# One modulation group on TensorE and early loads for another, in the lead-in of a two-layer hybrid decoder trunk

## The chip, the cores and the metric

The kernel runs on one core of a Trainium2 chip. The core has engines that run side by side, each with its own instruction stream: PE (TensorE, matrix products; the trace lists its weight loads apart, as PEld), DVE (VectorE), ACT (ScalarE), POOL (GpSimd), and SP, which here only issues transfers (DMA). The metric is the device time of one execution in microseconds (us), less is better. Three executions of the kernel before took 2290.22 to 2292.53 us, with a median of 2290.46.

## The reference

Two layers over x of 1024 tokens by 1024 channels, then a final RMSNorm. What matters for the change is the head of a layer:

```python
c_act = jax.nn.silu(c)                       # one conditioning vector of 1024
mod = c_act @ w_ada + b_ada                  # 3072 numbers for each layer
shift, scale, gate = jnp.split(mod[:, None, :], 3, axis=-1)
h = rms_norm(x, norm_g) * (1.0 + scale) + shift
proj = h @ w_in                              # all inputs of the three mixers
...                                          # pooling, retention, RWKV-7, merge
return x + gate * (merged @ w_out)
```

So no product of the first layer can start before the shift and scale of at least some channels are there, and `w_ada`, a matrix of 1024 by 3072, has to be multiplied by a single vector for them.

## The kernel before

x lies transposed: eight tiles of 128 channels (kt = 0 to 7), in two halves of 512 tokens each (h = 0, 1). A product of float32 accuracy is made from three fast ones: both operands are split into a high and a low part (hhi, hlo for the normalised x; two parts of a weight tile), and high by high, low by high and high by low are added up in PSUM.

The lead-in (`lead_in`, lines 1809 to 1895) brings the first layer to the point where its first three items, the columns called lora, k and r of head 0, are projected. `mms(h, kt)` makes the nine products of one x tile with those three items; 16 such calls, 144 products, are the lead-in's work on PE. They add up in six PSUM accumulators: three of the pool `acc` for h = 0, and `ch` and the two banks of `two` for h = 1. Before `mms(h, kt)` can run, `normed(h, kt)` (DVE) multiplies the x tile by the token's inverse root mean square, `affine(h, kt)` (ACT, two instructions) applies scale and shift for hhi and for x itself, and `low` (POOL) makes hlo. The sums over squares that the root mean square needs are `sq(h)`: ACT squares, DVE adds, PE sums over partitions by products with a column of ones. `rstd` and `rstd_bc` make the inverse root and spread it over a PSUM bank, from which `normed` reads. `one(h, kt)` is all of it for one tile.

Shift and scale come from six modulation groups. Groups 0 to 3 hold the shift and scale of x tiles 0, 1, 2 and 3, with four weight tiles of 128 x 512 each; groups 4 and 5 those of tiles 4, 5 and 6, 7, with eight weight tiles each. A group is computed by `ada` (line 695): eight steps on DVE, one for each 128 rows of `w_ada`, each of which multiplies a weight tile by a number per partition and adds it to a running sum in PSUM (`ada_ps`, the last step writes `ada_acc`). Then PE sums over the partitions with one-column products into `sums`, a PSUM bank shared by all these little sums (`small`, line 688), and `ada_end` makes `mod` and `acoef` on DVE. `coef(g)` runs a whole group. There is a second way, `ada_columns` (line 722), which the kernel before defines and, with `COLUMNS = ()`, doesn't use: PE multiplies each 128 x 128 block of the weights by a column of c, adds over the eight blocks in PSUM, and DVE has only `ada_end` to do.

The weight tiles of the groups live in borrowed buffers. Groups 0 and 1 fill the eight slots of a ring in tile G (`wada_slot`, the names `ringG`). Groups 2 and 3 use the `wh` and `wl` buffers, three of each, so that the last two of their eight tiles wait until group 2 has read its first two (`wada`). Group 4 takes the ring again as groups 0 and 1 free it (`aload(4, 8)`), and group 5 takes each ring slot as group 4 frees it: `astep(4, 5)` issues one step of group 4 and then one load for group 5. Other buffers of the lead-in: `ri` has 14 tiles, seven of which hold x of the second half; `r8` has four tiles of 128 x 2048, three of which hold the split weights of the first three items (`wbig`). The fourth `r8` tile is taken at the lead-in's end by `wprep(True)`, for the split weights of the next item. Raw weights arrive in three `wr` buffers.

The order of the work is not that of the code. Every call is recorded as an `Op` in `Log`, with its dependencies; a PSUM tensor counts by whole banks (`pieces`, line 157). `Log.plan` (line 333) then plays the whole program with assumed durations, transfers included, and picks at each point, for each engine, the ready operation with the lowest key, which is its place in the code plus a bias for its kind. Operations of the lead-in and of the RWKV chain count as urgent; a pending urgent one can hold back a longer one that isn't. A buffer is given in the order in which the code asks for it, once its earlier user is done. Some subtractions may be given to DVE or POOL, whichever is free by the plan. `emit` writes the instructions in the order of planned start times, each engine's and SP's queue included, and since `emit` issues them all, nearly every instruction has line 539 in the profile; the tile names tell them apart. The rope tables (`ang`, `nrot`, `over`), a job of DVE for the retention mixer, are not urgent and are slipped in where DVE is free by the plan.

Of the kernel before, what the change touches and what calls it, by code (L numbers as in the profile page):

```python
# [9 lines left out]
F32 = mybir.dt.float32  # L10
# [7 lines left out]
P = 128  # L18
# [4 lines left out]
HF = 512  # L23
# [67 lines left out]
    ADA.append((_c, [_c + _i for _i in range(4)], _n))  # L91
    _n += 8
FIRST = [("lora",), ("k", 0), ("r", 0)]
COLUMNS = ()
TWICE = (1, 2)
EARLY = (0, 0, 0, 2, 4)


# [454 lines left out]
def trunk_kernel(ctx, tc, xT, cvec, pos, vecs, consts, w_ada, w_all, pool_w, lora_w, out):  # L553
    nc = Log(tc.nc, tc)

    def pool(name, bufs, **kw):
        return PoolProxy(nc, ctx.enter_context(tc.tile_pool(name=name, bufs=bufs, **kw)), bufs, "")
# [3 lines left out]
    wp = pool("wp", 2)  # L561
# [18 lines left out]
    def nm(s):  # L580
        uid[0] += 1
        return f"{s}_{uid[0]}"

    def slot(tag, n, w=HF):
        def f(s, dt=F32):
            return (tp if w == HF else mp).tile([P, w], dt, tag=tag, name=nm(s), bufs=n)

        return f
# [3 lines left out]
    t_ri = slot("ri", 14)  # L592
# [24 lines left out]
    def r8(s):  # L617
        return rp.tile([P, 2048], F32, tag="r8", name=nm(s))
# [53 lines left out]
    def cond_act():  # L672
        cth = sp.tile([P, 8], F32, tag="mn", name=nm("cth"))
        nc.scalar.activation(cth, cact, AF.Tanh, scale=0.5)
        nc.vector.tensor_scalar(cth, cth, 0.5, 0.5, op0=ALU.mult, op1=ALU.add)
        nc.vector.tensor_tensor(cact, cact, cth, op=ALU.mult)
        nc.scalar.activation(fixed[:, 3:4], ones, AF.Sqrt)

    def ada_load(l, g, slot_, ws, n):
        for _ in range(n):  # L680
            w = slot_("wada")
            nc.sync.dma_start(out=w, in_=w_ada[l, ADA[g][2] + len(ws)])
            ws.append(w)

    sums_ps = []
    aw = [[] for _ in range(6)]

    def small(n):
        if not sums_ps:
            sums_ps.append([mx("sums"), 0])  # L690
        t, o = sums_ps[0]
        sums_ps[0][1] = o + n
        return t[:, o : o + n]

    def ada(l, g, slot_, gap=2200, acc_=t_lt, ws=None):
        n = len(ADA[g][1])
        W_ = n * P
        acc = acc_("ada_acc")[:, 0:W_]
        late = ws is None
        ws = [] if late else ws  # L700
        part = acc if late else mx("ada_ps")[:, 0:W_]
        for kt in range(NKT):
            i, o = divmod(kt * W_, HF)
            if late and o == 0:
                ada_load(l, g, slot_, ws, min(i + 2, 2 * n) - len(ws))
            w = ws[i][:, o : o + W_]
            if kt == 0:
                nc.vector.tensor_scalar_mul(part, w, cact[:, 0:1])
            else:
                nc.vector.scalar_tensor_tensor(  # L710
                    part if kt < NKT - 1 else acc, w, cact[:, kt : kt + 1], part, op0=ALU.mult, op1=ALU.add
                )
            yield gap
        if late:
            yield wait(acc)
        ps = mx("adaps") if late else small(n)
        for m in range(n):
            mmul(ps[:, m : m + 1], acc[:, m * P : (m + 1) * P], ones)
        ada_end(l, g, ps)
        yield  # L720

    def ada_columns(g):
        c, cols, _ = ADA[g]
        n = len(cols)
        ps = small(n)
        for m in range(n):
            for kt in range(NKT):
                i, o = divmod(kt * n * P, HF)
                mmul(
                    ps[:, m : m + 1], aw[g][i][:, o + m * P : o + m * P + P], cact[:, kt : kt + 1],  # L730
                    start=kt == 0, stop=kt == NKT - 1,
                )
        ada_end(0, g, ps)
# [233 lines left out]
    def plan_layer(l):  # L967
# [4 lines left out]
        while done < 4 or prog.get((l, 3), 0) < 10 or pools:  # L972
# [7 lines left out]
            elif pools and 4 - len(pools) <= done and len(lanes["mix"]) < 2:  # L980
                yield from pools.popleft()
            elif 24 - len(gates) < EARLY[done]:
                yield gates.popleft()
# [68 lines left out]
    def acc_ps():  # L1052
        return ps_a.tile([P, HF], F32, tag="acc", name=nm("acc"))
# [655 lines left out]
    def xdma(h, *kts):  # L1709
        for kt in kts:  # L1710
            xt = (mi if h == 0 else t_ri if kt < 7 else t_rk)("x")
            nc.sync.dma_start(out=xt, in_=xT[kt, h])
            xin[h].append(xt)
# [3 lines left out]
    def sq(h, *kts):  # L1717
        for kt in kts:
            t = mo("sq")
            nc.scalar.square(t, xin[h][kt])  # L1720
            if kt == 0:
                ssp[h] = small(4)
            if kt == 0 and TWICE[h] or kt % 2 == 0 and TWICE[h] == 1:
                prev = t
                continue
            if TWICE[h]:
                nc.vector.tensor_tensor(t, t, prev, op=ALU.add)
                prev = t
            if TWICE[h] == 2 and kt < 7:
                continue  # L1730
            for m in range(4):
                mmul(
                    ssp[h][:, m : m + 1], t[:, m * P : (m + 1) * P], ones,
                    start=kt == (1, 7)[TWICE[h] - 1] and m == 0, stop=kt == 7 and m == 3,
                )
# [22 lines left out]
    def normed(h, *kts, eng=None):  # L1758
        for kt in kts:
            if (h, kt) in isnorm:  # L1760
                continue
            isnorm.add((h, kt))
            x = xin[h][kt]
            if eng is None:
                nc.vector.tensor_tensor(x, x, rbc[h], op=ALU.mult)
            else:
                eng.tensor_tensor(x, x, rbs[h], op=ALU.mult)

    def affine(h, kt):
        x = xin[h][kt]  # L1770
        b, a = mod[0][:, SHIFT[kt] : SHIFT[kt] + 1], acoef[0][:, kt : kt + 1]
        hi, lo = hb("hhi"), hb("hlo")
        nc.scalar.activation(hi, x, AF.Identity, bias=b, scale=a)
        nc.scalar.activation(x, x, AF.Identity, bias=b, scale=a)
        h_cur[h].append((hi, lo))

    def low(eng, h, kt):
        hi, lo = h_cur[h][kt]
        eng.tensor_tensor(lo, xin[h][kt], hi.bitcast(F32), op=ALU.subtract)
# [3 lines left out]
    def wdma(j, *tiles):  # L1783
        for i in tiles:
            if j == 0:
                wbig.append(r8("wbig"))
            wraw[j, i] = wp.tile([P, HF], F32, tag="wr", name=nm("wr"), bufs=3)
            nc.sync.dma_start(out=wraw[j, i], in_=w_all[0, i, j])
# [16 lines left out]
    def steps(g, n):  # L1805
        for _ in range(n):
            next(g)

    def lead_in():
        V, G_ = nc.vector, nc.gpsimd  # L1810
        gs = [ada(0, g, None, ws=aw[g]) for g in range(6)]

        def aload(g, n):
            ada_load(0, g, wada_slot, aw[g], n)

        def both(kt, eng=None):
            for h in range(2):
                affine(h, kt)
                low(eng or G_, h, kt)

        def astep(g, nxt=None):
            for _ in range(8):
                steps(gs[g], 1)
                if nxt is not None:
                    aload(nxt, 1)

        cond_act()
        xdma(0, *range(8))
        nc.sync.dma_start(out=vec[0][:, 0:NVEC], in_=vecs[0])
        aload(0, 4)  # L1830
        nc.sync.dma_start(out=cst, in_=consts[:, 0 : CST["bone"]])
        wdma(0, 0)
        xdma(1, 0, 1, 2, 3)
        wdma(0, 1, 2)
        aload(1, 4)
        xdma(1, 4, 5, 6, 7)
        for g, n in ((2, 4), (3, 4)):
            for _ in range(n):
                w = wp.tile([P, HF], F32, tag=("wh", "wl")[_ % 2], name=nm("wada"), bufs=3)
                ada_load(0, g, lambda _: w, aw[g], 1)  # L1840
        def coef(g):
            if g in COLUMNS:
                ada_columns(g)
            else:
                steps(gs[g], 9)

        def one(h, kt):
            normed(h, kt)
            affine(h, kt)
            low(G_, h, kt)  # L1850
            mms(h, kt)

        acc6[0] = [acc_ps() for _ in range(3)]
        derive(0)
        sq(0, *range(8))
        rstd(0)
        rstd_bc(0)
        coef(0)
        wsp(0, 0, 1, 2)
        one(0, 0)  # L1860
        coef(1)
        one(0, 1)
        sq(1, *range(8))
        rstd(1)
        rstd_bc(1)
        coef(2)
        acc6[1] = [ps_c.tile([P, HF], F32, tag="ch", name=nm("acc")), cyt(), cyt()]
        normed(0, *range(3, 8))
        one(0, 2)
        wdma(1, 0, 1, 2)  # L1870
        aload(4, 8)
        normed(1, *range(8))
        one(1, 0)
        one(1, 1)
        coef(3)
        one(0, 3)
        one(1, 2)
        wsp(1, 0, 1, 2)
        astep(4, 5)
        steps(gs[4], 1)  # L1880
        one(0, 4)
        one(1, 3)
        one(0, 5)
        coef(5)
        one(1, 4)
        one(0, 6)
        one(1, 5)
        one(0, 7)
        one(1, 6)
        one(1, 7)  # L1890
        wprep(True)
        wprep()
# [486 lines left out]
```

## Time and profile before

| | |
|---|---|
| median of three executions | 2290.46 us |
| profiled execution | 2293.27 us |
| its span, first to last instruction | 2291.2 us |
| PE, PEld busy | 2249.2 us (98%), 1865.2 us (81%) |
| DVE, ACT, POOL busy | 1633.0 us (71%), 910.5 us (40%), 624.3 us (27%) |
| mean granted clock of TensorE | 0.993 |
| moved by DMA | 248.84 MB, 109 GB/s over the span |

All numbers below this table come from one profiled execution, on its own clock that starts with the span. The profile gives busy times for stretches of the span, lists instructions in order of time with the idle time ahead of each and what ended it, and groups instructions by the names of their output and inputs: `acc<-hhi,wbig` is a product of hhi with a weight tile of wbig into an accumulator. `x8` means eight records in a row. A product of plain float32 operands stands as two records. A busy PE isn't PE at its peak, since products overlap; the ends are modelled, and starts are the better measure of their rate. The granted clock is a share of TensorE's full rate.

### The profile page before, as it was taken

Reading aid. Unit: us, or ns where it says so; the run is one execution under the profiler, and the core shown is the slowest. Engines: PE = TensorE matmul, PEld = TensorE weight load, DVE = VectorE, ACT = ScalarE, POOL = GpSimd, SP = SyncE. Lnnn points to the kernel's source line nnn. Section 1 sums busy time; section 2 is a strip of 40 time slices with the busy share of each in tenths; the row PEclk is TensorE's granted clock in tenths of the full one; section 3 lists DMA queues with packets and bytes.
Section 4 is the critical chain, followed back from the end, with each engine's and each line's share of the span. In section 5 each row is a group of like instructions: output and inputs, shape, how many; then the busy total and the mean of one; then the engine's idle time right before and its main releaser. Section 6 shows DMA issues by size and latency. Waiting matters only on the chain.

```text
span 2291.2 us, 35095 instructions
## 1 busy us (share of the span) xinstructions
PE 2249.2 (98%) x13048; PEld 1865.2 (81%) x13048; DVE 1633.0 (71%) x2911; ACT 910.5 (40%) x1673; POOL 624.3 (27%) x549
## 2 busy tenths in 40 slices
PE   6999999999999999999999999999999999999998
PEld 5788888888888888888888888887888888888888
DVE  7996886878888754668667778688785844465854
ACT  5743433434234344323454344243432444442243
POOL 4132323323325210322122232332432500041311
PEclk8999999999999999999999999999999999999999
DMA  8221111112356642755540111111122533257442
GB/s 303 94 56 55 33 47 33 53 47 75 120 160 196 220 138 88 234 180 167 166 147 28 47 33 39 56 39 47 47 68 82 188 119 112 88 163 231 132 132 83
DMA packets 138042, 248.84 MB, mean 109 GB/s; under 512 B 15632, under 2 KB 18960, under 8 KB 137872
## 3 DMA queue, kind: packets, MB, share of 16 engines
q1 hardware_dynamic: 137872, 246.61, 33.3%
q8 instruction: 102, 1.67, 0.3%
q14 instruction: 68, 0.56, 0.1%
HBM read 187.04 MB, written 59.51 MB: 108 GB/s over the span
## 4 chain that ended last, share of the span: by engine, by line
PE 89%; DVE 5%; issue 1%; ACT 1%; POOL 0%; DVEq 0%; POOLq 0%
PE acc L539 74%; PE two L539 3%; PE ch L539 3%; PE av L539 1%; PE g L539 1%; PE ro L539 1%; PE bt L539 1%; PE rkv L539 1%; PE m L539 1%; DVE G L539 1%; PE lw L539 1%; PE rs L539 0%; PE pps L539 0%; DVE two L539 0%; DVE tm L539 0%
## 5 line engine op out<-in xcount | busy, mean ns | idle before, releaser
L539 PE MATMUL acc<-hhi,wh 128*128 128x512 f32 x1488 | 599.1, 403 | 0.0
L539 PE MATMUL acc<-hlo,wh 128*128 128x512 f32 x1488 | 598.5, 402 | 0.0
L539 PE MATMUL acc<-hhi,wl 128*128 128x512 f32 x1488 | 596.1, 401 | 0.0
L539 POOL TENSOR_TENSOR wl<-wr,wh 128x512 fp32r<-128x512 f32 x175 | 237.1, 1356 | 568.1 <-ACT wh L539 469.8
L539 PEld LDWEIGHTS acc<-hhi,wl 128*128 128x128 f32 x1488 | 280.9, 189 | 50.0 <-issue 1.1
L539 PEld LDWEIGHTS acc<-hhi,wh 128*128 128x128 f32 x1488 | 280.5, 189 | 50.4 <-issue 1.5
L539 PEld LDWEIGHTS acc<-hlo,wh 128*128 128x128 f32 x1488 | 280.8, 189 | 48.8 <-issue 0.7
L539 ACT CAST wh<-wr 128x512 fp32r<-128x512 f32 x242 | 149.2, 617 | 292.2 <-PE acc L539 234.7
L539 PE MATMUL acc<-T,wh 128*128 128x512 f32 x576 | 177.3, 389 | 0.0
L539 PEld LDWEIGHTS acc<-T,wh 128*128 128x128 f32 x576 | 108.1, 188 | 22.4
L539 DVE TENSOR_TENSOR wl<-wsum,wh 128x512 fp32r<-128x512 f32 x75 | 54.0, 720 | 93.3 <-ACT wh L539 92.9
L539 ACT COPY y<-two 64x128 f32<-64x128 f32 x128 | 32.9, 257 | 214.5 <-PE two L539 211.1
L539 PE MATMUL acc<-T,wl 128*128 128x512 f32 x288 | 112.1, 389 | 0.0
L539 DVE SCALAR_TENSOR_TENSOR S<-ch,pc,SP 64x64 f32<-64x64 f32 x256 | 72.0, 281 | 55.3 <-PE ch L539 49.1
L539 POOL TENSOR_TENSOR oz<-ol,oz 128x512 fp32r<-128x512 f32 x10 | 14.0, 1397 | 327.6 <-DVE wl L539 258.9
L539 ACT CAST wh<-wsum 128x512 fp32r<-128x512 f32 x96 | 59.6, 620 | 96.5 <-PE acc L539 93.5
L539 DVE TENSOR_TENSOR xst<-two,MT 64x128 f32<-64x128 f32 x128 | 37.5, 293 | 69.9 <-PE two L539 47.1
L539 DVE TENSOR_TENSOR two<-two,tm 64x30 f32<-64x30 f32 (+14 forms) x240 | 78.9, 329 | 7.0
L539 DVE TENSOR_TENSOR tm<-MT,two 64x30 f32<-64x30 f32 (+14 forms) x240 | 76.4, 318 | 8.5 <-ACT two L539 1.6
L539 DVE TENSOR_TENSOR wl<-wraw,wh 128x512 fp32r<-128x512 f32 x53 | 36.6, 690 | 62.4 <-ACT wh L539 62.4
L539 PE MATMUL acc<-oy,wh 128*128 128x512 f32 x256 | 79.7, 392 | 0.0
L539 PE MATMUL acc<-oG,wh 128*128 128x512 f32 x256 | 79.0, 390 | 0.0
(326 smaller groups left out, 4907.2 us busy)
## 6 DMA issues: line engine op xcount, KB each, us to landing
wr<-in_w_all SPq DMA_DIRECT2D x268, 256.0 KB, 2.7
wraw<-in_w_all SPq DMA_DIRECT2D x96, 256.0 KB, 2.7
gd<-gsg SPq DMA_DIRECT2D x96, 256.0 KB, 2.0
gs<-gd SPq DMA_DIRECT2D x96, 256.0 KB, 4.0
wada<-in_w_ada SPq DMA_DIRECT2D x72, 256.0 KB, 3.0
ol<-od SPq DMA_DIRECT2D x48, 256.0 KB, 3.5
traw<-hd SPq DMA_DIRECT2D x32, 256.0 KB, 3.0
ringG<-in_w_ada SPq DMA_DIRECT2D x24, 256.0 KB, 5.2
```

Of the source, the lines that this page charges most:

```text
L539: o.inst = f(*a, **k)
```

## The change

Three things change, all in the lead-in of the first layer. Group 1 is computed by `ada_columns` on PE instead of by eight steps on DVE. The last two weight tiles of group 3 get `ri` tiles in place of `wh` and `wl` ones. And the eight weight tiles of group 5 get buffers of their own, the fourth `r8` tile cut in four and four more `ri` tiles, with their loads issued right behind those of group 4; group 4's steps then run without loads between them. The ring in G serves groups 0, 1 and 4 only.

```diff
-COLUMNS = ()
+COLUMNS = (1,)
 TWICE = (1, 2)
+SPARE = ((3, 2), (3, 3))
...
         for g, n in ((2, 4), (3, 4)):
             for _ in range(n):
-                w = wp.tile([P, HF], F32, tag=("wh", "wl")[_ % 2], name=nm("wada"), bufs=3)
+                w = t_ri("wada") if (g, _) in SPARE else wp.tile([P, HF], F32, tag=("wh", "wl")[_ % 2], name=nm("wada"), bufs=3)
                 ada_load(0, g, lambda _: w, aw[g], 1)
...
         one(0, 2)
         wdma(1, 0, 1, 2)
         aload(4, 8)
+        more = r8("wada")
+        more = [more[:, i * HF : (i + 1) * HF] for i in range(4)] + [t_ri("wada") for _ in range(4)]
+        for w in more:
+            ada_load(0, 5, lambda _: w, aw[5], 1)
         normed(1, *range(8))
         one(1, 0)
         one(1, 1)
...
         one(1, 2)
         wsp(1, 0, 1, 2)
-        astep(4, 5)
-        steps(gs[4], 1)
+        steps(gs[4], 9)
         one(0, 4)
```

What group 1 now runs, unchanged from the kernel before:

```python
def ada_columns(g):
    c, cols, _ = ADA[g]
    n = len(cols)
    ps = small(n)
    for m in range(n):
        for kt in range(NKT):
            i, o = divmod(kt * n * P, HF)
            mmul(
                ps[:, m : m + 1], aw[g][i][:, o + m * P : o + m * P + P], cact[:, kt : kt + 1],
                start=kt == 0, stop=kt == NKT - 1,
            )
    ada_end(0, g, ps)
```

## The prediction

> **What bounds the kernel now.** I read the page first, then busy time by stretches, because the change touches only the first 80 us.
>
> ```profile
> span 2291.2 us, 35095 instructions
> 20.00:62.00 42.00, 30.93 (x109) 23.94 (x110) 37.45 (x75) 21.59 (x33) 21.71 (x19) 0.79 0.86 302
> 62.00:80.00 18.00, 18.00 (x78) 14.73 (x77) 17.03 (x30) 14.48 (x24) 3.09 (x8) 0.92 0.42 147
> 80.00:140.00 60.00, 57.85 (x353) 46.10 (x352) 56.65 (x85) 37.47 (x58) 14.38 (x14) 1.00 0.10 29
> 140.00:2291.20 2151.20, 2132.34 (x12468) 1770.85 (x12466) 1511.76 (x2697) 824.43 (x1540) 581.06 (x499) 1.00 0.33 105
> 28.00:44.00 16.00, 13.80 (x40) 10.81 (x41) 12.37 (x30) 9.57 (x16) 9.44 (x9) 0.50 0.93 337
> 90.00:120.00 30.00, 29.16 (x157) 22.97 (x156) 29.76 (x42) 19.29 (x29) 7.42 (x7) 1.00 0.11 31
> ```
>
> The columns are the stretch, its length, the busy time of PE, PEld, DVE, ACT and POOL, the granted clock, the DMA share and GB/s. From 62 us to the end PE is busy almost throughout: it idles 2.15 us in 80 to 140 and 2151.20 - 2132.34 = 18.86 us in all the rest. Between 20 and 62 it idles 11.07 us. So what comes off the end of the lead-in should come off the total, unless later work hands it back. The place for it is the stretch 20 to 62, where DVE is busy 37.45 of 42 us. The instructions there, in order of time, tell why PE waits:
>
> ```profile
> 20.69 2.92 PE L539 MATMUL acc<-hhi,wbig 128*128 128x512 f32 x6 [1.63 <-ACT hhi L539]
> 25.30 0.61 PE L539 MATMUL sums<-fixed,ada_acc 128*128 128x1 f32 x4 [0.82 <-DVE ada_acc L539]
> 28.29 0.59 PE L539 MATMUL sums<-fixed,sq 128*128 128x1 f32 x2 [2.39 <-DVE sq L539]
> 52.43 2.06 PE L539 MATMUL acc<-hhi,wbig 128*128 128x512 f32 x7 [2.03 <-ACT hhi L539]
> 61.47 2.93 PE L539 MATMUL acc<-hhi,wbig 128*128 128x512 f32 x6 [3.00 <-ACT hhi L539]
> 64.19 1.15 PE L539 MATMUL acc<-hlo,wbig 128*128 128x512 f32 x3
> 65.18 1.30 PE L539 MATMUL acc<-hhi,wbig 128*128 128x512 f32 x5
> 70.65 1.83 PE L539 MATMUL acc<-hhi,wbig 128*128 128x512 f32 x7
> 72.32 0.39 PE L539 MATMUL two<-hhi,wbig 128*128 128x512 f32 x1
> ...
> 80.02 0.62 PE L539 MATMUL two<-hlo,wbig 128*128 128x512 f32 x2
> ...
> 19.70 0.48 DVE L539 TENSOR_SCALAR ada_ps<-ringG,fixed 128x256 f32<-128x256 f32 x1
> ...
> 27.36 0.15 DVE L539 SCALAR_TENSOR_TENSOR acoef<-mod,vec 128x1 f32<-128x1 f32 x1
> ...
> 34.33 0.18 DVE L539 RECIPROCAL rn<-rn 128x4 f32<-128x4 f32 x1 [1.15 <-ACT rn L539]
> 36.68 1.28 DVE L539 TENSOR_TENSOR x<-x,two 128x512 f32<-128x512 f32 x2 [0.75 <-PE two L539]
> 39.74 0.69 DVE L539 TENSOR_TENSOR x<-x,two 128x512 f32<-128x512 f32 x1 [0.81 <-PE two L539]
> 41.31 2.48 DVE L539 TENSOR_TENSOR x<-x,two 128x512 f32<-128x512 f32 x4 [0.89 <-DMA hd<-x]
> 43.71 0.48 DVE L539 TENSOR_SCALAR ada_ps<-wada,fixed 128x256 f32<-128x256 f32 x1
> 45.16 3.10 DVE L539 SCALAR_TENSOR_TENSOR ada_ps<-wada,fixed,ada_ps 128x256 f32<-128x256 f32 x6
> 57.16 0.75 DVE L539 TENSOR_SCALAR ada_ps<-ringG,fixed 128x512 f32<-128x512 f32 x1
> 60.40 0.16 DVE L539 SCALAR_TENSOR_TENSOR acoef<-mod,vec 128x2 f32<-128x2 f32 x1
> 60.48 2.33 DVE L539 SCALAR_TENSOR_TENSOR ada_ps<-ringG,fixed,ada_ps 128x512 f32<-128x512 f32 x3
> 64.60 0.75 DVE L539 SCALAR_TENSOR_TENSOR ada_acc<-ringG,fixed,ada_ps 128x512 f32<-128x512 f32 x1
> ```
>
> The number in brackets is idle time ahead of the instruction and what ended it. DVE runs the modulation groups one after another: group 3 from 43.71, group 4 behind it, group 5 from 57.16 to 64.60 + 0.75 = 65.35. Group 4's coefficients stand at 60.56, ACT makes the first operand from them, and PE, which had waited 3.00 us, starts at 61.47 on the 36 products of x tiles 4 and 5, then runs without a gap through the 36 of tiles 6 and 7, of which the last lie at 80.02. So the DVE chain up to group 4 sets the end of the lead-in; group 5 is just in time behind it (its steps begin with no wait at 57.16).
>
> **Group 1 to PE.** On DVE eight steps of 128x256 go. Six such steps took 3.10 us (45.16), 0.517 each: 8 x 0.517 = 4.1 us off the chain ahead of coef(4). They lay between 19.70 and the sums at 25.30; the chain behind them moves up.
>
> On PE come 2 columns x 8 tiles = 16 products of a 128x128 weight with one column, two records each in this trace (the lead-in has 16 + 4 sums over squares of this form, and the trace 40 records of them), so 32 records. The nearest row is the same form, back to back:
>
> ```profile
> 8.69 5.28 PE L539 MATMUL sums<-fixed,sq 128*128 128x1 f32 x24 [0.52 <-DVE sq L539]
> L539 PEld LDWEIGHTS sums<-fixed,sq x40: 288/333/338, 6.3 to 33.6; 128*128 128x128 f32 x40
> ```
>
> 5.28 / 24 = 0.22 each, 7.0 us in all. The lower end is the row at 25.30 (0.61 / 4 = 0.15, 4.9 us), the upper end a weight load of 0.333 us with nothing overlapped, 10.7 us. I take 7.0, the row of the same form. They go into the stretch up to 28.29, where PE idled 1.63 + 0.82 + 2.39 = 4.84 us, and group 1's four sum records (0.61) go: 7.0 - 4.84 - 0.61 = 1.55 us more than the cover. What is queued behind: all these sums share one PSUM bank, which the planner treats as one, so the products wait until DVE has read group 0's sums, and the second half's sums over squares (28.29) wait until DVE has read group 1's. Behind those stand rn, the reciprocal, the broadcast and normed(1) on DVE (36.68). I charge the 1.55 us to this path (ends 0, if the second half's squares are late anyway, and 10.7 - 4.84 - 0.61 = 5.25). If group 1's coefficients come later than the 27.51 of before (27.36 + 0.15), the products of (0,1) come later too; they have the wait at 52.43 behind them as cover.
>
> **The two tiles of group 3 (SPARE) and the eight of group 5.**
>
> ```profile
> 19.05 3.71 SPq L539 DMA_DIRECT2D wada<-in_w_ada  x6
> ...
> 32.78 0.96 SPq L539 DMA_DIRECT2D wada<-in_w_ada  x2
> ...
> 50.27 1.00 DVE L539 CAST ang<-posi 128x512 f32<-128x512 int32 x1
> 53.68 1.21 DVE L539 TENSOR_SCALAR ang<-ang,cst 128x512 f32<-128x512 f32 x1
> 59.88 0.42 DVE L539 TENSOR_SCALAR nrot<-ang 128x512 f32<-128x512 f32 x1
> 62.72 1.18 DVE L539 TENSOR_SCALAR nrot<-nrot 128x512 f32<-128x512 f32 x1
> ...
> 43.69 1.12 ACT L539 CAST wbig<-wr 128x512 fp32r<-128x512 f32 x2
> 45.11 2.54 POOL L539 TENSOR_TENSOR wbig<-wr,wbig 128x512 fp32r<-128x512 f32 x2
> 75.92 0.69 ACT L539 ACTIVATE lt<-acc,vec 128x511 f32<-128x511 f32 x1
> ```
>
> Group 3's last two tiles are asked for at 32.78, since they wait for group 2 to free two wh/wl buffers; with ri buffers they follow the six at 19.05. Then all of group 3 (8 steps, 4.1 us) is there to fill DVE's waits of 1.15 + 0.75 + 0.81 + 0.89 = 3.6 us between 33 and 41.3, and it needs less time after normed(1). Ends 0 and 3.6; I take 3.6, since 4.1 us of ready work covers it.
>
> Group 5's eight loads move up behind aload(4, 8). On SP and on the DMA engines eight more loads of 256 KB stand there: 3.71 / 6 = 0.62 us each, 4.9 us. Behind them on SP stand the raw weights of the item after the first three, the positions and the first stores of hd. Those weights are cast at 43.69 and first needed once an accumulator is free, after 75.92; that slack hides 4.9 us. If it were gone, the 4.9 us would stand. Group 5 waited for no load, so the earlier loads give nothing by themselves: 0, and I leave a better fill of DVE for the range.
>
> The tile of r8 that takes four of them was the one for those weights. Their cast (1.12) and subtraction (2.54) now come after group 5's first four steps, which in the old places end near 61.3: 61.3 + 3.7 = 65, ahead of 75.92 by 11 us. Cost 0. The t_ri tiles (7 for x, 2, 4 of 14) are free again before the rwkv work asks for them; 0.
>
> **What is late next.** If coef(4) moves up by about 6 us, PE's wait of 3.00 goes or shrinks, and the half-rate start goes with it: nine products from 61.47 to 65.18 took 3.71 us, seven from 70.65 to 72.32 took 1.67 (0.24 each), so 3.71 - 2.16 = 1.55 us come off. Against that, the four rope instructions that slipped in between groups 4 and 5 (1.00 + 1.21 + 0.42 + 1.18 = 3.8 us) may come after the lead-in, where DVE is busy 29.76 of 30 us and PE already loses 0.84. Ends 0 and 3.8; I take half, 1.9.
>
> **Sum.** -4.1 (DVE steps) - 3.6 (DVE waits) + 1.55 (PE columns) - 1.55 (half rate) + 1.9 (rope) = -5.8 us. The profiled execution took 2293.27 us (span 2291.2 and 2.07 around it), 2.81 above the median of 2290.46. 2293.27 - 5.8 = 2287.5, and against the median 2284.7.
>
> **Rule against row.** In 28 to 44 the granted clock is 0.50 with PE busy 13.80 of 16 us, after an idle of only 2.39 us; at 52.43 an idle of 2.03 leaves the rate full, at 61.47 one of 3.00 halves it. The Trainium skill (TensorE: Matmul & The Clock Gate, "Why this matters for your kernels") says that gaps beyond about 3 us between bursts drop the clock to half, and that some 4 us of steady work bring it back. By that rule the trace agrees at 52.43 and 61.47, while the drop near 28 came after a shorter gap. By the rule the columns, filling 17 to 28, would keep the later products at full rate, and the sum would be the clock rival's below.
>
> **Rivals.**
> Full clock: the one-column products leave PE no gap before 28, so the 13.80 us at 0.50 take half, 6.9 us less. For it: the longest gap there is exactly where they go. Against it: PE in that stretch waits for ACT and DVE, so its rate is not what ends it. It decides if PE runs without a gap from about 37 us on. 2284.7 - 6.9 = 2277.8.
>
> Hidden: the loads change nothing (no step of groups 3 or 5 waited for one), and only the 4.1 us count, less 1.55 for the columns and 1.9 for rope work: -0.65, 2289.8. For it: DVE at 29.76 of 30 in 90 to 120. Against it: PE has products in hand there.
>
> Slower: the whole program's order is written from planned start times, so an earlier lead-in gives another order for the other 2150 us. PE idles 18.86 us there; the order at hand may be a good one by chance. It decides when that idle time grows by over 5.8 + 4.6 = 10.4 us, by more than half. With 12 us more: 2296.7. For it: each DVE and POOL choice hangs on those times. Against it: the work and its due times are the same, and 140 us already show PE fed.
>
> **How the numbers follow.** 0.2%, 4.6 us, is about what a measurement of this kernel tells from no change. The forecast, 2280.5 to 2287.5, gets 0.50; full clock 0.13; hidden 0.21; slower 0.16. Of the forecast's half some 0.07 lies above 2285.9. So faster 0.43 + 0.13 = 0.56, same 0.07 + 0.21 = 0.28, slower 0.16. The range runs from below full clock, 2277, to 2294, which leaves out most of the slower case.
>
> **What would show it.** Right: no group 1 steps on DVE; 32 more one-column records between 17 and 31; group 3's steps before or among normed(1); coef(4) near 55; no 3 us gap ahead of tiles 4 and 5; rope instructions moved behind; the last two-products near 74. Wrong: normed(1) later than 38 us behind the columns, a gap before the v item for want of its r8 tile, or PE idle after 140 well over 18.86 us.

## The result, and the profile after

The changed kernel took 2287.8 us (median of 22 executions, 2284.59 to 2290.24), the kernel before on the same chip 2291.7 us (22 executions, 2289.05 to 2294.06). The ratio is 0.9982, with a 95% interval of 0.9976 to 0.9989: 3.9 us less, by the interval 2.5 to 5.5. The forecast was 5.8 us less and 2284.7, the range 2277 to 2294.

The profiled execution of the changed kernel took 2284.81 us, 3.0 under its median, and that of the kernel before 2293.27, 1.6 above its own. So the two traces lie 8.5 us apart where the medians lie 3.9 apart. What follows here shows where the time goes in this pair; only part of it is there on average.

The page's first lines and busy time by stretches, changed kernel (columns as in the prediction):

```profile
span 2282.9 us, 35125 instructions
PE 2246.9 (98%) x13076; PEld 1866.6 (82%) x13076; DVE 1627.5 (71%) x2907; ACT 907.4 (40%) x1671; POOL 623.8 (27%) x545
...
20.00:62.00 42.00, 35.20 (x152) 28.65 (x152) 38.78 (x78) 24.24 (x36) 13.63 (x13) 0.88 0.82 294
62.00:80.00 18.00, 17.05 (x82) 13.38 (x80) 13.97 (x20) 15.54 (x26) 6.64 (x10) 1.00 0.45 134
80.00:140.00 60.00, 59.27 (x361) 48.41 (x360) 58.94 (x97) 34.11 (x56) 15.50 (x17) 1.00 0.15 42
140.00:2282.90 2142.90, 2124.43 (x12440) 1765.39 (x12438) 1505.70 (x2688) 821.08 (x1534) 583.66 (x496) 1.00 0.33 105
28.00:44.00 16.00, 12.05 (x49) 9.26 (x50) 13.37 (x31) 9.10 (x13) 7.51 (x6) 0.79 1.00 354
```

PE's idle time goes from 2291.2 - 2249.2 = 42.0 to 2282.9 - 2246.9 = 36.0 us: 11.07 to 6.80 in 20 to 62, 0 to 0.95 in 62 to 80, 2.15 to 0.73 in 80 to 140, 18.86 to 18.47 in all the rest. PE's busy time falls by 2.3 us although products were added. In the same trace the granted clock in 28 to 44 is 0.79 where it was 0.50, so more of the lead-in's products ran at full rate.

DVE and PE in order of time, changed kernel:

```profile
31.95 0.49 DVE L540 TENSOR_SCALAR ada_ps<-wada,fixed 128x256 f32<-128x256 f32 x1
...
34.15 0.18 DVE L540 RECIPROCAL rn<-rn 128x4 f32<-128x4 f32 x1 [0.66 <-ACT rn L540]
...
36.91 1.28 DVE L540 TENSOR_TENSOR x<-x,two 128x512 f32<-128x512 f32 x2
38.12 0.47 DVE L540 SCALAR_TENSOR_TENSOR ada_acc<-wada,fixed,ada_ps 128x256 f32<-128x256 f32 x1
...
42.25 1.28 DVE L540 TENSOR_TENSOR x<-x,two 128x512 f32<-128x512 f32 x2 [0.60 <-PE two L540]
...
43.52 0.74 DVE L540 TENSOR_SCALAR ada_ps<-ringG,fixed 128x512 f32<-128x512 f32 x1
...
54.95 0.15 DVE L540 SCALAR_TENSOR_TENSOR acoef<-mod,vec 128x2 f32<-128x2 f32 x1
```

```profile
18.88 1.41 PE L540 MATMUL sums<-fixed,ringG 128*128 128x1 f32 x6
...
22.99 0.42 PE L540 MATMUL sums<-fixed,ringG 128*128 128x1 f32 x2
...
25.04 2.73 PE L540 MATMUL sums<-fixed,ringG 128*128 128x1 f32 x24
29.82 1.44 PE L540 MATMUL sums<-fixed,sq 128*128 128x1 f32 x6 [2.04 <-DVE mod L540]
...
56.01 2.92 PE L540 MATMUL acc<-hhi,wbig 128*128 128x512 f32 x6 [2.23 <-ACT hhi L540]
...
77.83 0.62 PE L540 MATMUL two<-hlo,wbig 128*128 128x512 f32 x2
...
88.51 0.39 PE L540 MATMUL acc<-hhi,wh 128*128 128x512 f32 x1
```

The rows of the kernel before that answer to them and were not shown yet: a cast between group 3's steps, the last step of group 3, the first of group 4, and the first product of the item after the next, which reads `wh`:

```profile
44.10 1.13 DVE L539 CAST bone<-braw 128x128 fp32r<-128x128 f32 x1
...
48.30 0.48 DVE L539 SCALAR_TENSOR_TENSOR ada_acc<-wada,fixed,ada_ps 128x256 f32<-128x256 f32 x1
48.81 0.75 DVE L539 TENSOR_SCALAR ada_ps<-ringG,fixed 128x512 f32<-128x512 f32 x1
...
94.85 0.39 PE L539 MATMUL acc<-hhi,wh 128*128 128x512 f32 x1
```

The place where the gain arises is seen here. `normed(1)` on DVE ends at 43.53, as it did before (43.79, by the row at 41.31). Before, group 3 stood behind it, from 43.71 to 48.78, and group 4 began at 48.81. Of these 5.1 us, 4.1 are group 3's eight steps and 1.0 is the cast `bone`, which took 1.13 us there and takes 0.22 in the changed kernel, behind group 4's first step. Now group 3 runs from 31.95 to 38.59, in and ahead of `normed(1)`, and group 4 begins at 43.52, right behind it: 5.3 us earlier. The coefficients of group 4 come 60.40 - 54.95 = 5.45 us earlier, the first product of tiles 4 and 5 moves from 61.47 to 56.01, and the `wh` item (its first product) from 94.85 to 88.51, 6.3 us earlier.

### The profile page after: what moved, and what is told of

Same layout as the page of the kernel before. It is cut to its first block, busy times and chain, and to the rows that moved or that the text cites. A ratio compares the mean times of both kernels' runs of the same rounds, so it can differ in the third digit from the quotient of the medians.

```text
span 2282.9 us, 35125 instructions
## 1 busy us (share of the span) xinstructions
PE 2246.9 (98%) x13076; PEld 1866.6 (82%) x13076; DVE 1627.5 (71%) x2907; ACT 907.4 (40%) x1671; POOL 623.8 (27%) x545
## 4 chain that ended last, share of the span: by engine, by line
PE 89%; DVE 8%; issue 1%; ACT 1%; DMA 0%; POOL 0%; SPq 0%; DVEq 0%; POOLq 0%; ACTq 0%
PE acc L540 73%; PE two L540 3%; PE ch L540 3%; PE av L540 1%; PE ro L540 1%; PE g L540 1%; DVE two L540 1%; DVE tm L540 1%; DVE ksq L540 1%; PE lw L540 1%; PE m L540 1%; PE rkv L540 1%; PE bt L540 1%; DVE G L540 1%; PE rs L540 0%
```

## The experiments

The change has three parts: group 1 on PE (C below), the two spare tiles for group 3 (S), and the early loads of group 5 in buffers of their own (G). The table has, for each kernel, when the coefficients of groups 1 to 5 stand (start of `acoef` on DVE), the first `wh` product, the median, and the ratio to the kernel before on the same chip. There the kernel before took 2291.57 to 2292.22 us in the median.

| kernel | groups 1, 2, 3, 4, 5 | `wh` | median | ratio (95%) |
|---|---|---|---|---|
| before | 27.36, 38.77, 51.37, 60.40, 69.53 | 94.85 | 2291.7 | |
| changed (C+S+G) | 29.80, 36.33, 44.18, 54.95, 63.94 | 88.51 | 2287.8 | 0.9982 (0.9976 to 0.9989) |
| e1: C | 30.08, 37.23, 51.46, 59.33, 68.66 | 97.89 | 2294.88 | 1.0013 (1.0004 to 1.0022) |
| e3: S | 27.10, 36.63, 50.87, 59.54, 69.13 | 94.24 | 2294.72 | 1.0014 (1.0005 to 1.0023) |
| e2: S+G | 27.22, 37.93, 52.16, 60.74, 69.51 | 94.54 | 2292.13 | 1.0006 (0.9997 to 1.0015) |
| e8: C+G | 30.51, 37.75, 54.19, 62.71, 73.30 | 97.45 | 2304.86 | 1.0054 (1.0040 to 1.0067) |
| e10: C+S | 30.17, 37.12, 50.09, 58.88, 68.07 | 92.64 | 2293.35 | 1.0006 (0.9997 to 1.0014) |
| e4: C+S+G, group 3 on PE too | 30.56, 38.00, 55.43, 58.02, 69.59 | 94.37 | 2293.98 | 1.0007 (0.9998 to 1.0015) |
| e9: C, rope tables later | 29.38, 36.64, 50.72, 58.60, 69.03 | 93.64 | 2297.5 | 1.0025 (1.0016 to 1.0034) |
| e7: C+S+G, order of the rest shaken | 29.31, 35.67, 43.52, 55.14, 65.28 | 87.37 | 2364.8 | 1.0317 (1.0303 to 1.0331) |
| h1: lead-in of C+S+G, rest as before | 30.14, 37.38, 47.99, 59.19, 72.63 | 102.49 | 2300.81 | 1.0034 (1.0022 to 1.0046) |
| h2: lead-in as before, rest of C+S+G | 27.14, 38.27, 50.80, 59.32, 67.33 | 94.67 | 2294.01 | 1.0010 (1.0001 to 1.0019) |
| h4: lead-in of C, rest as before | 30.59, 37.83, 53.57, 61.60, 71.19 | 96.50 | 2294.24 | 1.0011 (1.0002 to 1.0020) |
| h8: C+G, rest as before | 29.59, 36.09, 51.89, 60.41, 71.01 | 95.20 | 2299.72 | 1.0036 (1.0022 to 1.0049) |

No kernel beat the changed one. Of its parts, C and S were run alone and all three pairs were run; none of these beat the kernel before. G was not run alone.

### e1: group 1 to PE alone

```diff
-COLUMNS = ()
+COLUMNS = (1,)
```

> The kernel before with group 1 on PE alone; all loads as before. Theory (the sum): DVE's chain loses eight steps, 4.1 us, and the columns hand back at most 1.55 on the way to normed(1), since group 3 can't fill DVE's waits without its last two tiles: 2 to 3 us faster than before, coef(4) near 57.5. Rival A (the columns are all of it): as fast as the changed kernel, about 4 us under before. Rival B (the loads carry it): within 1 us of before.

Measured: 2294.88, slower by 2.7 us, which none of the expectations had. The eight DVE steps are gone, yet group 3's coefficients come no earlier (51.46 against 51.37), and group 4's only 1.07 us earlier (59.33 against 60.40). DVE of this kernel, in order of time:

```profile
34.53 1.51 DVE L539 SCALAR_TENSOR_TENSOR ada_ps<-wada,fixed,ada_ps 128x256 f32<-128x256 f32 x3
...
37.80 1.88 DVE L539 TENSOR_TENSOR x<-x,two 128x512 f32<-128x512 f32 x3 [0.41 <-PE two L539]
...
43.35 1.28 DVE L539 TENSOR_TENSOR x<-x,two 128x512 f32<-128x512 f32 x2 [0.59 <-PE two L539]
44.55 1.01 DVE L539 SCALAR_TENSOR_TENSOR ada_ps<-wada,fixed,ada_ps 128x256 f32<-128x256 f32 x2
```

Four of group 3's steps go ahead of `normed(1)`, which ends at 44.63 (43.35 + 1.28), and four stay behind it, mixed with other work. Then ACT is late. PE and ACT of this kernel:

```profile
85.29 1.28 ACT L539 ACT_TABLE_LOAD   x1
...
87.33 0.50 PE L539 MATMUL nps<-ksh,bone 128*128 128x512 f32 x1 [3.28 <-ACT sg L539]
```

A sine for the rope tables (`nrot`), with a load of ACT's function table ahead of it and one behind, now stands ahead of `sg` of the RWKV chain, and PE waits 3.28 us for that. So the term "8 x 0.517 = 4.1 us off the chain ahead of coef(4)" doesn't hold by itself: 1.07 of the 4.1 arrived.

### e3, e2 and e10: which parts belong together

```diff
+SPARE = ((3, 2), (3, 3))          # e3; e2 adds group 5's early loads, e10 adds COLUMNS = (1,)
...
-                w = wp.tile([P, HF], F32, tag=("wh", "wl")[_ % 2], name=nm("wada"), bufs=3)
+                w = t_ri("wada") if (g, _) in SPARE else wp.tile([P, HF], F32, tag=("wh", "wl")[_ % 2], name=nm("wada"), bufs=3)
```

> The kernel before with ri tiles for group 3's last two weight tiles and nothing else. Theory: this is what lets group 3 fill DVE's waits, so all that the early loads give is here: the same as the kernel with both sets of early loads, within 1 us. Rival: group 5's early loads give the gain by freeing DVE's order of steps; then this one is within 1 us of before.

> The changed kernel with group 1 back on DVE; the early loads for groups 3 and 5 stay. Theory: group 3's steps fill DVE's waits of 3.6 us between 33 and 41, but the chain keeps its eight steps of group 1, so 1 to 3 us faster than before, coef(4) near 57. Rival A: within 1 us of before, since no step of groups 3 and 5 waited for a load. Rival B: about 4 us under before.

> Columns for group 1 and ri tiles for group 3, with group 5 loaded as in the kernel before. Theory now (the two only work together: with group 1 off DVE there is time ahead of normed(1), and with its tiles there group 3 has work for it): group 3's coefficients come near 44 instead of 51, and the gain is that of the changed kernel, 3 to 5 us under before; group 5's early loads are worth less than 1 us. Rival: group 5's loads are the third part without which nothing is won; then within 1.5 us of before.

Measured: 2294.72 for S, 2292.13 for S+G and 2293.35 for C+S. For S neither theory came (2.6 us slower than before); S+G took the time of the kernel before, as its rival A had it; C+S stayed within 1.5 us of it, as its rival had it. With S alone group 3's tiles are there, but DVE has no room for them before `normed(1)`, since group 1's steps are still on it. C+S has the room and the tiles, and still group 3 is not early (50.09). DVE and SP's queue of C+S, in order of time:

```profile
32.73 0.69 DVE L540 TENSOR_SCALAR omu<-vec 128x13 f32<-128x13 f32 x1
...
34.62 0.15 DVE L540 TENSOR_SCALAR vec<-vec 128x28 f32<-128x28 f32 x1
...
26.43 0.33 SPq L540 DMA_DIRECT2D vec<-in_vecs  x1
```

and the same of the changed kernel:

```profile
44.38 0.17 DVE L540 TENSOR_SCALAR omu<-vec 128x13 f32<-128x13 f32 x1
...
47.63 0.68 DVE L540 TENSOR_SCALAR vec<-vec 128x28 f32<-128x28 f32 x1
...
32.99 0.33 SPq L540 DMA_DIRECT2D vec<-in_vecs  x1
```

In C+S only three steps of group 3 stand ahead of `normed(1)`, and two small preparations of vectors stand among them. In the changed kernel the transfer that those read is asked for 6.6 us later, behind group 5's loads; they come after `normed(1)`, and all of group 3 goes ahead. At the `wh` mark the three parts are seen to be needed together: the changed kernel is 6.3 us early there, C+S 2.2, S 0.6, S+G 0.3, and C and C+G are late. The totals show it less cleanly, because S, S+G, C+S and C+G also have another order of the later work (see e7). That the displaced transfer is what tipped the planner is the likeliest reading, and h1 below supports it, but nothing else was varied to prove it.

### e8: the change without the spare tiles

```diff
-SPARE = ((3, 2), (3, 3))          # against the changed kernel
+SPARE = ()
```

> The changed kernel with group 3's last two tiles back in wh and wl; columns and group 5's early loads stay. Theory: group 3 can't move ahead of normed(1), so it loses what the two tiles give, 1.5 to 3.6 us slower than the changed kernel, 1 to 2.5 us under before. Rival: equal to the changed kernel within 1 us, since no step waited for these tiles.

Measured: 2304.86, slower by 12.7 us, more than either expectation. Group 3's last two tiles now wait behind group 5's in SP's queue. The first of them is asked for here, where it was at 32.78 in the kernel before:

```profile
37.84 0.33 SPq L540 DMA_DIRECT2D wada<-in_w_ada  x1
```

Group 3's coefficients come at 54.19 and PE waits 3.57 us ahead of tiles 4 and 5. At the `wh` item the kernel is 2.6 us late (97.45 against 94.85); most of the 12.7 is lost later, which h8 takes up.

### e4: one group more on PE

```diff
-COLUMNS = (1,)
+COLUMNS = (1, 3)
```

> The changed kernel with group 3 on PE as well as group 1. DVE loses eight more steps, 4.1 us; PE gains 32 records at 0.114 us as the warm ones of the changed kernel took, 3.6 us, mostly in its gaps. Theory (DVE's chain to group 4 sets the end): coef(4) near 51, PE's wait of 2.23 us before tiles 4 and 5 gone with its half-rate start, 2 to 4 us faster than the changed kernel. Rival (PE is the bound by now): within 1 us of it, or slower by up to 3.6.

Measured: 2293.98, 6 us more than the changed kernel. The theory had it 2 to 4 us faster, and the rival at most 3.6 slower, so neither came. Group 4 comes no earlier (58.02), and group 3's coefficients stand at 55.43, 11 us later than with DVE. Once group 3 was in front of `normed(1)`, DVE had nothing more to give there.

### e9: the rope tables later

```diff
     def rope_tables():
-        yield 15000
+        yield 26000
```

(on top of e1, so that the sine no longer stands ahead of `sg`)

> Columns alone, with the rope tables' start put off from 15 to 26 us of the planner's clock, so that their sine with its two activation-table loads no longer stands on ACT ahead of the first sigmoid of the RWKV chain. In the run with columns alone PE waited 3.28 us there and then ran at half rate. Theory (that wait is what made columns alone slower): 3 to 4.5 us faster than columns alone, 1 to 2 us under before. Rival (the order of all the rest does it): no faster than columns alone, within 1 us.

Measured: 2297.5, ratio 1.0025 (1.0016 to 1.0034). That is 2.6 us more than e1, and neither expectation. The wait of 3.28 us is gone and the lead-in's lateness with it: the `wh` item starts at 93.64, 1.2 us earlier than before. But from about 800 us of the trace the kernel is 5.3 us late. In the traces, after 220 us, some 3300 of PE's 11,934 records stand at another place in the order than in the kernel before. The cause in e1 was right for the place; the remedy cost more elsewhere.

### e7: what another order of the rest costs

```diff
-SHAKE = 0
+SHAKE = 200
```

(against the changed kernel; the keys of all work that isn't urgent are shifted a little, at random, and the lead-in's order stays the same to its last products)

> The changed kernel with the planner's keys shaken a little for everything that isn't urgent; the lead-in's order is the same to its last products, the rest comes in another order. It measures the price of another order, the slower rival of the prediction. If an order is worth little: within 1.5 us of the changed kernel. If the rival is real: 3 to 12 us off it, up rather than down, with PE's idle time after 140 us above 18.5.

Measured: 2364.8, ratio 1.0317 (1.0303 to 1.0331), 77 us more than the changed kernel: the rival, and far beyond the 3 to 12 us that it was given. The lead-in is as early as the changed kernel's (`wh` at 87.37). After 140 us:

```profile
140.00:2361.40 2221.40, 2160.22 (x12454) 1770.73 (x12452) 1495.19 (x2688) 818.03 (x1537) 609.64 (x519) 0.99 0.32 101
```

PE idles 61 us where it idled 18.5. So the order at hand is worth far more than the change. The traces show who keeps it, by the order of the instructions after 220 us. In the changed kernel and e1 it is the order of the kernel before: of PE's 11,934 records 15 and 4 stand elsewhere, of DVE's 2562 one and none, of ACT's and POOL's none. In e3, e10 and e4 some 1200 of PE's records stand elsewhere, in e2 and e8 some 2700.

### h1, h2 and h4: one kernel's lead-in with another's order of the rest

```diff
-        return sorted(done, key=lambda o: (o.start, o.idx))
+        return self.replay(todo, last, seen)   # the lead-in by its own planned starts, all other work by a list of starts
```

> The changed kernel's lead-in (all three parts, in its own planned order), and behind it the instructions of the rest in the order that the kernel before plans for them, written out as a list. Theory A (the total is the shift of the lead-in plus what the order of the rest is worth; the order of the changed kernel gave about nothing): the first product of the item after the lead-in near 88.5, as in the changed kernel (88.51, 94.85 before), its head start kept to the end, 2286 to 2289, 3 to 6 us under the kernel before. Theory B (the gain is the new order of the rest, and the lead-in's shift is handed back with the old order): 2291 to 2293, and the marks after 140 us as in the kernel before.

> The other way round: the lead-in of the kernel before, and behind it the rest in the order that the changed kernel plans. Theory A: 2290 to 2294, within 2 us of the kernel before, the first product of the next item near 94.9, PE's idle time after 140 us near 18.5 to 19. Theory B: 2286 to 2289, at or near the changed kernel's time, with the head start coming up somewhere after 140 us.

> The lead-in with only group 1 moved to PE (in its own planned order), and the rest in the order of the kernel before. With the order that it plans for itself this part alone took 2294.88, 2.7 us more than the kernel before, its last two-products 0.85 us earlier but the first product of the next item 3.0 later, behind a sine for the rope tables on ACT. Theory A: with the old order of the rest the sine stands elsewhere, and the 0.85 us are what is left: 2290.5 to 2292. Theory B (the columns themselves cost something that this kernel keeps, or the order is not what made it slower): 2294 to 2296 again.

Measured: 2300.81 for the changed lead-in with the old order of the rest, 2294.01 the other way round, 2294.24 for e1's lead-in with the old order. h1 lies outside both theories, h2 at the edge of the first, and h4's 2294.24 is e1's time again, as the second had it: the halves don't add up (+8.9 and +2.1 us, where the whole is -3.9). h1 shows why. "The rest" isn't all later: some of its work fills the lead-in. DVE, ACT, PE and SP of h1:

```profile
35.48 0.87 DVE L625 TENSOR_SCALAR omu<-vec 128x13 f32<-128x13 f32 x1
...
70.70 0.69 DVE L625 TENSOR_TENSOR lw<-lraw,lw 128x512 fp32r<-128x512 f32 x1 [4.56 <-ACT lw L625]
...
70.04 0.62 ACT L625 CAST lw<-lraw 128x512 fp32r<-128x512 f32 x1 [3.60 <-DMA lraw<-in_lora_w]
...
76.19 2.50 PE L625 MATMUL acc<-hhi,wbig 128*128 128x512 f32 x5 [5.38 <-ACT hhi L625]
...
25.07 0.33 SPq L625 DMA_DIRECT2D vec<-in_vecs  x1
```

With the transfer of the vectors early again, the preparations stand ahead of `normed(1)` again, and group 3's coefficients come at 47.99 in place of 44.18. And a weight of the RWKV chain, `lw`, that was right where it stood in the old lead-in, is now waited for by ACT (3.60 us for its transfer) and by DVE (4.56 us), with group 5's coefficients queued behind it; PE loses 5.38 us there. One and the same lead-in, in the same planned order, makes the program 4 us faster or 9 slower by what stands between its instructions.

### h8: e8 with the old order after 200 us

Here the own order is kept for all that is planned before 200 us; from there on the work stands in the order of the kernel before, written out as in h1.

> Group 1 on PE and group 5's early loads, without the two spare tiles for group 3 (2304.86 with the order that it plans for itself, 12.9 us more than the kernel before in the profiles, 4.5 of them by the mark at 174 us). Up to 200 us of planned time its own order is kept; from there on the instructions stand in the order of the kernel before. Theory A (the later 8 us are the price of another order of the rest; the lead-in itself costs only 4 to 5): 2295.5 to 2298, and the lateness by mark stays near 4.5 us to the end. Theory B (a late lead-in grows later by itself, whatever the order): 2303 to 2306 again, with the lateness growing between 178 and 720 us.

Measured: 2299.72, ratio 1.0036 (1.0022 to 1.0049): 5.1 us less than e8, between the two expectations. Two marks, the first of the `rs` products and of the final norm, in the kernel before, e8 and h8:

```profile
236.09 1.05 PE L539 MATMUL rs<-rq,rk 128*128 128x128 f32 x8
...
2236.60 2.48 DVE L539 TENSOR_TENSOR fin<-xres,rbc 128x512 f32<-128x512 f32 x4 [0.64 <-PE rbc L539]
```

```profile
241.58 1.05 PE L540 MATMUL rs<-rq,rk 128*128 128x128 f32 x8
...
2249.51 2.48 DVE L540 TENSOR_TENSOR fin<-xres,rbc 128x512 f32<-128x512 f32 x4 [0.64 <-PE rbc L540]
```

```profile
240.22 1.05 PE L625 MATMUL rs<-rq,rk 128*128 128x128 f32 x8
...
2241.78 2.48 DVE L625 TENSOR_TENSOR fin<-xres,rbc 128x512 f32<-128x512 f32 x4 [0.64 <-PE rbc L625]
```

e8 is 5.5 us late at the first mark and 12.9 at the second, h8 4.1 and 5.2. So of the 7.4 us that e8 loses in between, all but 1.1 belong to its order of the rest. What h8 has left is 5.2 us in these traces, of which 4.1 stand by 240 us: its late lead-in and the place where the two orders meet (2.3 us late at 176 us, 4.1 at 240). In the medians it is 8 us. The trace of the kernel before lies 1.6 us above its median, which accounts for part of the difference; the rest is open.

## Why the prediction came out as it did

**The time.** 2287.8 lies in the range, 3.1 above the forecast. Part of that is the starting point, since the kernel before took 2291.7 here and not 2290.46; as a difference, 3.9 us came of 5.8. Of the three sides, 3.9 us less is just inside the 4.6 that I had called no change from a few runs; with 22 runs of each it is told from no change. It stands between the forecast and the hidden rival (2289.8).

**What holds it up.** That the DVE chain up to group 4 sets the lead-in's end, that the end of the lead-in passes to the total, and that PE's idle time after 140 us would stay (18.86 to 18.47) all came as put. Of the signs, `coef(4)` at 54.95 (near 55), group 3 among `normed(1)`, `normed(1)` at 36.91 (not later than 38) and no gap for want of the `r8` tile came: its weights are cast at 61.09 where it was 43.69, and nothing waits for them.

```profile
61.09 1.12 ACT L540 CAST wbig<-wr 128x512 fp32r<-128x512 f32 x2
...
70.24 0.69 ACT L540 ACTIVATE lt<-acc,vec 128x511 f32<-128x511 f32 x1
...
102.46 1.28 ACT L540 ACT_TABLE_LOAD   x1
```

The first half's accumulators are read at 70.24, where it was 75.92: 5.7 us earlier, which is nearly the forecast's 5.8 for this pair of traces. That agreement is luck in part: too much was put on the gains (7.7 us for DVE's work, where 5.3 came, and 1.55 for the half-rate start, where 0.15 came), and that was made up by costs that did not come (1.9 for rope work and most of 1.55 for the columns).

**-4.1 and -3.6, added up.** This is the step that failed. Both terms say that DVE work leaves the stretch ahead of group 4, but `normed(1)` is a fixed point in it: it starts when the second half's root mean square is there (36.68 before, 36.91 after), whatever DVE has spared. Across the other kernels it starts between 35.25 and 39.05. So what can come off is what stood behind it up to group 4, from 43.71 to 48.81: 5.1 us, not 7.7, and of these only 4.1 are group 3's steps; the other 1.0 is the cast `bone`. It measured 5.3. And it isn't two gains of which one may come without the other: C alone and S alone bring group 4 only 1.07 and 0.86 us earlier, and C+S 1.52. My reading that the early loads of group 5 "give nothing by themselves" was right (e2), and that they cost and give nothing beside the rest was wrong (C+S against all three: 1.0006 to 0.9982, 5.5 us, of which 4.1 stand at the `wh` item).

**+1.55 for the columns.** They took 1.41 + 0.42 + 2.73 = 4.56 us in this trace, 4.4 to 4.6 in four others, and 1.41 + 0.42 + 5.11 = 6.94 in five, so 7.0 was a fair price. As the prediction said could happen, work behind them came later: group 1's coefficients by 2.4 us (29.80 against 27.36), the products of x tile 1 by 2.4 (31.12 against 28.74), and the second half's sums over squares by 1.5 (29.82 against 28.29). But `rn` stands at 34.15 (34.33 before), and `normed(1)` starts 0.2 later. So on the path they cost 0.2 in this pair. Where they took 6.94 us, `normed(1)` started at 37.53 to 39.05, so there they may not have been free; other orders are mixed into that.

**-1.55 for the half-rate start.** PE's wait ahead of tiles 4 and 5 shrank from 3.00 to 2.23 us and the six products behind it took 2.92 us, as before (2.93). The nine products of the term took 3.71 us before and 3.56 now (56.01 to 59.57). So the term is -0.15.

**+1.9 for rope work.** The sign that the rope instructions move behind did not come: the four DVE steps stayed among those of groups 4 and 5 (51.77 to 60.33). But they took 0.42 + 0.48 + 0.42 + 0.42 = 1.7 us, where they had taken 3.8, so the loss did not come. Beside the long rows before, POOL was at work; whether that is the cause was not tested. The sine on ACT moved too: before, its table loads stood among the first steps of the RWKV chain; now the first is at 102.46, behind them.

```profile
89.77 1.28 ACT L539 ACT_TABLE_LOAD   x1
```

PE's idle time in 80 to 140 falls by 1.4 us, but not for the sine: 1.31 us of it lay at 82.83 to 86.35, ahead of that sine (91.06), and 0.95 us of new idle time stands at 77.49. By the marks of this pair of traces, group 4 begins 5.3 us earlier, its coefficients come 5.45 earlier and its first product 5.46. From that product to the `wh` item it took 33.38 us before and takes 32.50 now, 0.88 less: 0.36 by PE's waits on that way and 0.15 by the nine products, and the rest is not put down to anything. Together that is the 6.3 us.

**The last two-products** came at 77.83, not near 74: the operand for them was queued on ACT behind another table load, and PE did the next item's products first. A mark that other work can overtake is a poor one.

**The full-clock rival** came in part: products run at full rate from 35.4 us in this trace and from 44.4 in the kernel before. It did not come the way that the rival had it, since the clock dropped right behind the columns (at 28.33) and rose again later. As I had put against it, the end of that stretch is DVE's, and the gain stayed small.

**The slower rival**, another order of the rest, is real and large for this kernel (e7, e8, e9), and did not happen here, because the order is the same again from about 220 us on. I gave it 0.16 without having any row that tells it; only the orders of the two kernels beside each other do.

**What stays open.** The pair of traces says -8.5, the medians say -3.9. How much of the difference lies in the lead-in from execution to execution is not settled: the columns ran at two rates in different traces, and the time doesn't simply follow (in h4's trace they took 2.73 us, and it is 1.2 us over its median). Of the changed kernel's lead, 6.3 at the `wh` item, another 2 us are gained by the final norm in this pair, of which PE's idle time explains 0.4. That the displaced `r8` tile is free was read from rows; neither it nor G as a whole was tried alone.

## What to carry to other kernels

Work taken off an in-order engine helps only up to the next instruction that waits for something else; count what stands behind that point and can be brought ahead of it, and don't add the work removed to the waits filled. For that all must be there at once, room, data and buffers, so parts of such a change measured one by one can each look like a loss. And where a planner writes the order of everything, compare the two orders first: a difference that dies out after the place of the change promises that the gain is kept, and one that goes on can cost more than the change is worth.

## What the runs showed that was not expected

One-column products run at two rates. The same 24 records took 2.73 us in the changed kernel (0.114 each) and 5.11 in C+S (0.213 each), while the row of the granted clock says 1.00 for both. PE of C+S, then the stretches of h1, whose columns took 5.11 too:

```profile
24.83 5.11 PE L540 MATMUL sums<-fixed,ringG 128*128 128x1 f32 x24
...
31.49 2.48 PE L540 MATMUL acc<-hhi,wbig 128*128 128x512 f32 x5
```

```profile
28.00:32.00 4.00, 3.75 (x16) 3.60 (x17) 3.26 (x9) 1.63 (x2) 0.00 (x0) 1.00 1.06 385
```

In C+S five products of 512 columns took 2.48 us from 31.49, 0.46 from start to start, where it is 0.23 late in the lead-in; h1 is the same there, and its clock column says 1.00. So up to the first change that a trace records, the 1.00 is no sign of full rate: in the kernel before, too, the six products from 20.69 took 2.92 us at a clock of 1.00, as long as at the half-rate start at 61.47. The starts have to be read for it. By them PE came up to full rate just ahead of the 24 columns in five of the ten kernels that have them (2.73 us), and behind them, at 36 to 41 us, in the other five (5.11 us); what decides it isn't known. From the first change that a trace records on, the clock column and the starts agree.

And one-column products did not keep the rate up. In all five kernels with 2.73 us the clock fell 0.06 to 0.6 us after the last of these columns, when PE had hardly begun to wait. The trace of e9 shows it best; its columns end at 26.91:

```profile
24.20:26.90 2.70, 2.70 (x25) 2.63 (x23) 2.49 (x5) 0.07 (x1) 0.00 (x0) 1.00 1.05 386
26.90:27.00 0.10, 0.01 (x1) 0.00 (x0) 0.10 (x1) 0.00 (x0) 0.00 (x0) 0.83 1.11 410
27.00:29.40 2.40, 0.00 (x0) 0.00 (x0) 2.33 (x7) 0.00 (x0) 0.00 (x0) 0.50 1.06 379
```

By its rows PE was busy without a break from 22.58 to 26.91, and the clock fell at 26.97. The idle time of 2.49 us that follows is not what made it fall. Nor does the length of an idle time decide alone: half rate followed after 2.04 us (e1, at 52.51) and 2.22 (h2, at 51.87), and did not follow after 2.36 (e8, at 109.82) and 2.38 (h8, at 107.53). The Trainium skill (TensorE: Matmul & The Clock Gate, "Why this matters for your kernels") says that gaps beyond about 3 us between bursts drop the clock. Here it dropped after 2.04 us, and in e9 with no gap ahead of it. What the recorded changes do show is a fixed grid: in the changed kernel, by the clock column in narrow windows, they lie at 24.92, 28.33, 35.16, 55.64 and 59.05 us, each a whole multiple of 3.41 us from the next.
